# Sums of weight blocks for eight tiles of the second FFN made in HBM by accumulating transfers, and three more of its tiles by seven block products

## The chip, the cores and the metric

The kernel runs on one core of a Trainium2 chip. The metric is the device time of one execution in microseconds (us). The core's engines are named as in the profile: PE (TensorE, matrix products), PEld (its weight loads), DVE (VectorE), ACT (ScalarE), POOL (GpSimd) and SP (SyncE, which here only issues transfers). [...]

## The reference

A decoder trunk of two layers over 512 tokens of width 1024, all in float32. Layer 0 mixes tokens with a gated unit (mixer A), layer 1 with windowed attention (mixer B). Each layer then has a gated FFN with a short causal convolution, and an embedding added through a gate. What the change touches is the up projection of the FFN, `xn @ w_up`:

```python
def conv_ffn(xn, w_up, conv_w, conv_b, w_down):
    S = xn.shape[1]
    h = xn @ w_up                                   # (512, 1024) @ (1024, 5632)
    hp = jnp.pad(h, ((0, 0), (CONV_WIDTH - 1, 0), (0, 0)))
    c = conv_b + sum(hp[:, t:t + S] * conv_w[t] for t in range(CONV_WIDTH))
    g, u = jnp.split(c, 2, axis=-1)
    return (jax.nn.silu(g) * u) @ w_down
```

## The kernel before, in words

**Precision.** Every weight block is split into two float32r parts, `wh` (a cast on ACT, L203) and `wl` (the rest, a subtraction on DVE, L204), and so is every activation. A product is three matmuls: high by high, high by low, low by high (`mm3`, L224).

**Weights on their way.** All weight loads are a list of *pieces* in order of use, up to 1 MB each, and each piece is cut into *units* of up to 1024 columns (`plan` and its kin, L73 to L117). `load` (L168) issues a piece's transfer from SP into one of three staging buffers r0 to r2 of 8 KB per partition, taken in turn (`staged`, L149). `pump` (L179) splits units into four rotating pairs `wh`, `wl`, so splits run four units ahead of PE. A load therefore waits until the buffer three places back has been split. SP works in order: whatever waits on SP holds the loads behind it.

**FFN tiles.** The up projection of each layer runs in 22 tiles, numbered from 0 (`up`, L736): tile j yields 128 gate and 128 line features for 512 tokens. A plain tile has eight blocks of inputs by two outputs, 48 matmuls of 512 columns, and two units. A *woven* tile (`woven_up`, L786) pairs input blocks, cuts the tokens in halves, and forms the 2 x 2 block product with seven products instead of eight (Winograd's form of Strassen's scheme): 84 matmuls of 256 columns. For that it needs four blocks of the weights (0 to 3) and four sums of them. `weave` (L155) makes the sums on DVE into a second staging buffer (L163 to L165): s3 = w1 + w3, s0 = w1 + w0, s2 = s3 + w0, s1 = s2 + w2. A woven tile has three full units and a half one: (w0, w2), (s2, s3), (s0, s1), (w3). The products collect in two PSUM tiles `ux` and `uy`; ACT copies parts of them out (`head`, `side`, `tail`), DVE combines these (L811, L812), and `gated` (L753) applies convolution, silu and the product of gate and line. The copy `side` (L804) must be done before the last product into `uy` may begin, as that writes over it.

`UPS` lists the woven tiles, the same for both layers; `ASIDE` gives some of them another place in SBUF for `head` and `tail`.

**Order in an FFN.** `PARTS` cuts the tiles in (0, 8), (8, 16), (16, 22). Of the first two parts the down projection is woven too (`woven_add`, L593): it takes the part's activations and adds its results onto rows `saved` in HBM by accumulating transfers from POOL (L600). The first tile of the next part is computed ahead of it. So the order is: tiles 0 to 8, down projection, tiles 9 to 16, down projection, tiles 17 to 21, down projection.

**Before the FFN of layer 0**: mixer A's gate in four chunks (`u`, L1026 to L1047), its output projection (`woven_add` onto h), the embedding's projection (`ple_in`).

**Order on a queue.** Instructions are put in each engine's order by the framework; `behind(a, b)` (L143) adds that a comes after b in the order, without a wait.

Of the kernel before, what the change touches and what calls it, by code (L numbers as in the profile page):

```python
# [8 lines left out]
F32 = mybir.dt.float32  # L9
F32R = mybir.dt.float32r  # L10
AF = mybir.ActivationFunctionType
ALU = mybir.AluOpType

P = 128
D = 1024
S = 512
KD = D // P
# [2 lines left out]
NJ = FF // P  # L20
PARTS = [(0, 8), (8, 16), (16, 22)]
WOVEN = 2
UPS = (7, 8, 9, 10, 12, 14, 16, 17, 18, 20, 21)
ASIDE = {7: 12, 9: 7, 17: 7, 20: 6}
PAIRS = 4
SLOTS = 9
N = S // 2
# [25 lines left out]
def tile_yoco(ctx: ExitStack, tc: tile.TileContext, t, out: bass.AP, out_b: bass.AP):  # L53
    nc = tc.nc
# [9 lines left out]
    dram = ctx.enter_context(tc.tile_pool(name="dram", bufs=1, space=bass.MemoryType.DRAM))  # L64
# [3 lines left out]
        return mmp.tile([P, S], F32, tag="mm", name=name)  # L68


    pieces, paired, woven, beside = [], set(), set(), set()

    def plan(ap_, n, cols, own=None):  # L73
# [23 lines left out]
    def plan_woven(w, n_chunks, k0, k1):  # L97

        for c in range(n_chunks):
            n = (k1 - k0) * P  # L100
            woven.add(len(pieces))
            pieces.append((w[c, :, k0 * 256 : k1 * 256], 2 * n, [(0, n)] * 3 + [(0, n // 2)], None))

    def plan_ups(l, j0, j1):
        for j in range(j0, j1):
            (plan_woven if j in UPS else plan_cols)(t["w_up"][l, j : j + 1], 1, *((0, KD) if j in UPS else (KD,)))

    def plan_ffn(l):
        plan(t["pT"][l], 2 * S, S, own=[(mp, "m4", "m5")])
# [30 lines left out]
    raws, ready, splits, sums = {}, {}, {}, {}  # L140
    state = {"raw": 0, "unit": 0, "next": 0, "tags": [0, 1, 2], "turn": 2, "pt": 0, "sent": {}}

    def behind(ins, front):  # L143

        tc.add_manual_dep(ins.ins, front.ins.name,
                          mybir.DependencyInfo(mybir.DependencyClass.NoSync, mybir.DependencyReason.DATA),
                          reason="order")

    def staged(name):  # L149
        tags = state["tags"]  # L150
        r = wp.tile([P, 2 * UNIT], F32, tag=f"r{tags[state['turn'] % len(tags)]}", bufs=1, name=name)
        state["turn"] += 1
        return r

    def weave(i, q):  # L155


        n = pieces[i][1] // 4
        g = raws[i][:, : 4 * n].rearrange("p (k b m) -> p b k m", b=4, m=P)
        if q == 0:  # L160
            s = sums[i] = staged(f"wsum{i}")[:, : 4 * n].rearrange("p (b k m) -> p b k m", b=4, m=P)
            k = n // P
            nc.vector.tensor_add(s[:, 0::3], g[:, 1:2].to_broadcast([P, 2, k, P]), g[:, 0::3])  # L163
            nc.vector.tensor_add(s[:, 2], s[:, 3], g[:, 0])
            nc.vector.tensor_add(s[:, 1], s[:, 2], g[:, 2])  # L165
        return (g[:, 0:3:2], sums[i][:, 2:4], sums[i][:, 0:2], g[:, 3:4])[q]

    def load(upto, queue=nc.sync):  # L168
        while state["raw"] < min(upto, len(pieces)):
            j = state["raw"]  # L170
            a, m = pieces[j][:2]
            r = raws[j - 1][:, UNIT:] if j in beside else staged(f"wraw{j}")
            ins = queue.dma_start(r[:, :m].rearrange("p (c m) -> p c m", c=2) if j in paired else r[:, :m], a)
            for front in state["sent"].pop(j, []):
                behind(ins, front)
            raws[j] = r
            state["raw"] += 1
# [107 lines left out]
    minus_half = const.tile([P, S // 64], F32, name="minus_half")  # L285
# [37 lines left out]
    class Norm:  # L323
# [121 lines left out]
        def rstd(self):  # L445

            r = tp.tile([P, S], F32, tag="rstd", name=f"{self.name}rstd")
            if self.line is not None:
                nc.gpsimd.dma_start(r, self.line.partition_broadcast(P))
            else:  # L450
                nc.scalar.copy(r, self.spread(0, S // 64))
            return r

    def inv_root(ms, name, scale=1.0, n=None):
        if n is None:
            n = ms.shape[1]
            ms = [(slice(None), ms)]
        m = const.tile([P, n], F32, tag=f"ms{n}", bufs=2, name=f"{name}m")
        for some, x in ms:
            box["m"] = nc.vector.tensor_scalar(m[some, :], x, scale, EPS, op0=ALU.mult, op1=ALU.add)  # L460
        r = const.tile([P, n], F32, tag=f"rt{n}", bufs=2, name=f"{name}rt")
        nc.gpsimd.tensor_tensor(r, m, minus_half[:, :n], op=ALU.pow)
        return r

    box = {}
# [263 lines left out]
    def ffn(l, norm, nxt):  # L729
# [4 lines left out]
            behind(nc.sync.dma_start(saved[k], h[k]), box["squared", k])  # L734

        def up(j, later=False):  # L736
            if j in UPS:
                return woven_up(j, later)
            parts = chunk(256, KD)
            pss = [psum(f"up{j}_{s}") for s in range(2)]  # L740
            if j:
                for s in range(2):
                    mm3(pss[s], parts, xs, s * P)
            else:
                for k, ((wh, wl, off), (xh, xl)) in enumerate(zip(parts, xs)):
# [40 lines left out]
        def woven_up(j, later):  # L786

            product = products(ins)
            n = PAIRS * P
            chain, other = psum(f"ux{j}")[:, first], psum(f"uy{j}")  # L790
            if j in ASIDE:
                head, tail = couple(ASIDE[j], f"out{j}", F32)
            else:
                head, tail = (tp.tile([P, S], F32, tag="hs", name=f"{x}{j}") for x in ("gate", "line"))
            side = tp.tile([P, N], F32, tag="sq", name=f"side{j}")
            w = unit()
            product(1, chain, w, 0)
            behind(box["silu"], nc.scalar.copy(head[:, first], chain))
            product(2, other[:, first], w, n)
            w = unit()  # L800
            product(6, chain, w, 0, first=False)
            nc.scalar.copy(head[:, second], chain)
            product(5, other[:, second], w, n)
            nc.scalar.copy(side, other[:, second])  # L804
            w = unit()
            product(7, chain, w, 0, first=False)
            minus(tail[:, second], chain)
            product(3, other[:, second], w, n, first=False)
            product(4, chain, unit(), 0, first=False)
            minus(tail[:, first], chain)  # L810
            nc.vector.tensor_sub(tail[:, second], tail[:, second], side)  # L811
            nc.vector.tensor_add(head, head, other)  # L812
            return (head, tail) if later else gated(j, (head, tail))
# [7 lines left out]
        ins = inputs()  # L821
# [202 lines left out]
    edge = at.tile([P, PAIRS, 2, N], F32R, tag="vtl", name="edge")  # L1024
    us = [Pair(c, edge, f"us{c}", range(3 * PAIRS)) for c in range(PAIRS)]
    for c in range(4):  # L1026
        parts = chunk(256, KD)
        ups = [psum(f"u{c}_{j}") for j in range(2)]
        for j in range(2):
            mm3(ups[j], parts, xs, j * P)  # L1030
        for j in range(2):
            m = 2 * c + j
            ps = ups[j]
            z = tp.tile([P, S], F32, tag="hs", name=f"uz{m}")
            nc.vector.tensor_mul(z, ps, rstd)
            u = tp.tile([P, S], F32, tag="sg", name=f"u{m}")
            nc.scalar.activation(u, z, AF.Gelu_apprx_tanh)
            sp = psum(f"s{m}")
            for b in range(NC):
# [596 lines left out]
```

## Time and profile before

| | us |
|---|---|
| median of 3 runs (lowest to highest) | 1100.68 (1100.63 to 1100.82) |
| the profiled execution | 1100.31 |
| its span, first to last instruction | 1098.6 |
| mean granted clock of PE | 0.998 |

Where the parts of the kernel lie in the profiled execution, by the chain of waits:

| stretch | us from the span's start |
|---|---|
| mixer A's gate, four chunks | 49.8 to 98.7 |
| first FFN, tiles 0 to 8 | 153.7 to 252 |
| first FFN, tiles 9 to 16 | 290.8 to 375 |
| second FFN, tiles 9 to 16 | 838.6 to 923 |

How to read the profile: a row of the chain of waits or of the timeline has the start, the length, engine and line, and a count of instructions merged into it. A row of a group has line, engine and operation, output and inputs with shapes, count, then busy time, mean ns of one, idle time of the engine just before and what ended it. Matmuls are pipelined: their length in a group (389 ns for 512 columns, 283 for 256) is longer than the time from one to the next, so PE's cost is read from starts in the chain. A few matmul records can be missing from a trace. In a timeline a row of SP gives the issue of transfers, not their arrival.

### The profile page before, as it was taken

Reading aid. Unit: us, or ns where it says so; the run is one execution under the profiler, and the core shown is the slowest. Engines: PE = TensorE matmul, PEld = TensorE weight load, DVE = VectorE, ACT = ScalarE, POOL = GpSimd, SP = SyncE. Lnnn points to the kernel's source line nnn. Section 1 sums busy time; section 2 is a strip of 40 time slices with the busy share of each in tenths; the row PEclk is TensorE's granted clock in tenths of the full one; section 3 lists DMA queues with packets and bytes.
Section 4 is the critical chain, followed back from the end, with each engine's and each line's share of the span. In section 5 each row is a group of like instructions: output and inputs, shape, how many; then the busy total and the mean of one; then the engine's idle time right before and its main releaser. Section 6 shows DMA issues by size and latency. Waiting matters only on the chain.

```text
span 1098.6 us, 17575 instructions
## 1 busy us (share of the span) xinstructions
PE 1089.3 (99%) x6629; PEld 975.0 (89%) x6629; DVE 943.0 (86%) x1504; ACT 674.2 (61%) x1177; POOL 155.9 (14%) x228
## 2 busy tenths in 40 slices
PE   9999999999999999999999999999999999999997
PEld 7888988899998999988888887888999989999886
DVE  5598889999799978877988997799997999798886
ACT  5744666566676656655656775565666666567544
POOL 1200300002200030021114452000022000300200
PEclk9999999999999999999999999999999999999999
DMA  8621884126833388353224216441268333974534
GB/s 291 136 89 44 200 265 150 42 77 135 193 115 116 91 185 242 121 190 112 66 88 135 78 58 226 176 153 39 77 155 172 115 116 92 204 224 145 201 94 98
DMA packets 52693, 151.33 MB, mean 138 GB/s; under 512 B 13624, under 2 KB 21568, under 8 KB 42112
## 3 DMA queue, kind: packets, MB, share of 16 engines
q1 hardware_dynamic: 40560, 128.77, 36.3%
q0 software_dynamic: 10480, 16.78, 10.1%
q10 hardware_dynamic: 1568, 4.65, 1.1%
q8 instruction: 52, 0.85, 0.3%
q14 instruction: 33, 0.27, 0.1%
HBM read 116.89 MB, written 25.18 MB: 129 GB/s over the span
## 4 chain that ended last, share of the span: by engine, by line
PE 91%; DVE 3%; SPq 2%; issue 2%; ACT 1%; DMA 1%; POOL 0%; POOLq 0%; DVEq 0%; ACTq 0%
PE up L234 20%; PE ux L234 10%; PE dx L234 10%; PE uy L234 8%; PE dy L234 8%; PE q L234 4%; PE gate L234 4%; PE u L234 4%; PE o L234 4%; PE d L234 4%; PE up L749 2%; SPq L1393 2%; PE pv L1325 1%; PE v L244 1%; PE v L246 1%
## 5 line engine op out<-in xcount | busy, mean ns | idle before, releaser
L204 DVE TENSOR_TENSOR wl<-wraw,wh 128x1024 fp32r<-128x1024 f32 (+2 forms) x198 | 217.5, 1104 | 42.3 <-ACT wh L203 40.9
L203 ACT CAST wh<-wraw 128x1024 fp32r<-128x1024 f32 (+2 forms) x197 | 182.9, 933 | 108.2 <-PE up L234 21.8
L204 DVE TENSOR_TENSOR wl<-wsum,wh 128x1024 fp32r<-128x1024 f32 x84 | 102.4, 1227 | 38.1 <-ACT wh L203 37.3
L203 ACT CAST wh<-wsum 128x1024 fp32r<-128x1024 f32 x84 | 87.9, 1051 | 42.9 <-PE uy L234 14.5
L600 POOL DMA_DIRECT2D saved<-side x16 | 14.0, 873 | 404.2 <-ACT side L556 404.2
L761 DVE SCALAR_TENSOR_TENSOR c<-up,vec,c 128x511 f32<-128x511 f32 (+1 forms) x88 | 65.1, 745 | 2.4 <-ACT c L759 2.0
L234 PE MATMUL up<-nf10h,wh 128*128 128x512 f32 x160 | 62.3, 389 | 0.0
L234 PE MATMUL up<-nf00h,wh 128*128 128x512 f32 x160 | 62.3, 389 | 0.0
L234 PE MATMUL up<-nf10l,wh 128*128 128x512 f32 x160 | 62.3, 389 | 0.0
L234 PE MATMUL up<-nf00l,wh 128*128 128x512 f32 x160 | 62.3, 389 | 0.0
L234 PE MATMUL up<-nf00h,wl 128*128 128x512 f32 x160 | 62.1, 389 | 0.0
L234 PE MATMUL up<-nf10h,wl 128*128 128x512 f32 x160 | 62.0, 389 | 0.0
L759 ACT ACTIVATE c<-up,vec 128x512 f32<-128x512 f32 x44 | 34.0, 777 | 31.7 <-PE up L234 26.5
L163 DVE TENSOR_TENSOR wsum<-wraw 128x1024 f32<-128x1024 f32 x42 | 51.3, 1221 | 0.7
L234 PE MATMUL ux<-t,wh 128*128 128x256 f32 x264 | 50.4, 283 | 0.0
L234 PEld LDWEIGHTS ux<-t,wh 128*128 128x128 f32 x264 | 41.2, 192 | 0.0
L234 PE MATMUL ux<-t,wl 128*128 128x256 f32 x132 | 37.4, 283 | 0.0
L234 PEld LDWEIGHTS up<-nf10h,wl 128*128 128x128 f32 x160 | 30.0, 188 | 6.2
L234 PEld LDWEIGHTS up<-nf00h,wl 128*128 128x128 f32 x160 | 30.0, 188 | 6.2
L234 PEld LDWEIGHTS up<-nf10l,wh 128*128 128x128 f32 x160 | 30.1, 188 | 6.2
L234 PEld LDWEIGHTS up<-nf00l,wh 128*128 128x128 f32 x160 | 30.0, 188 | 6.1
L767 ACT ACTIVATE a<-c 128x512 f32<-128x512 f32 x44 | 27.8, 632 | 12.4 <-DVE c L761 12.4
(772 smaller groups left out, 3769.2 us busy)
## 6 DMA issues: line engine op xcount, KB each, us to landing
wraw<-in_w_up SPq DMA_DIRECT2D x44, 1024.0 KB, 5.4
wraw<-in_w_down SPq DMA_DIRECT2D x16, 1024.0 KB, 4.9
wraw<-in_w_gate SPq DMA_DIRECT2D x8, 1024.0 KB, 5.4
wraw<-in_w_down SPq DMA_DIRECT2D x8, 768.0 KB, 4.4
wraw<-in_w_u SPq DMA_DIRECT2D x4, 1024.0 KB, 9.4
wraw<-in_w_out SPq DMA_DIRECT2D x4, 1024.0 KB, 5.1
saved<-head POOLq DMA_DIRECT2D x16, 256.0 KB, 4.6
saved<-rest POOLq DMA_DIRECT2D x16, 256.0 KB, 6.9
```

What stands on the lines that cost most here:

```text
L163: nc.vector.tensor_add(s[:, 0::3], g[:, 1:2].to_broadcast([P, 2, k, P]), g[:, 0::3])
L203: cast = nc.scalar.copy(hi, src)
L204: state["split"] = splits[u] = cast, nc.vector.tensor_sub(low, src, hi.bitcast(F32))
L234: return [nc.tensor.matmul(ps, w, x, start=first and j == 0, stop=last and j == len(todo) - 1, skip_group_check=onto) for j, (w, x) in enu ...
L244: nc.tensor.matmul(ps, xh[:, s], wh[:, a:b], start=st, stop=False)
L246: nc.tensor.matmul(ps, xh[:, s], wl[:, a:b], start=False, stop=en)
L600: box["onto"] = nc.gpsimd.dma_start(x, y, accum_op=ALU.add)
L749: nc.tensor.matmul(ps, w[:, off + s * P : off + (s + 1) * P], x, start=k == 0 and x is xh and w is wh, stop=k == KD - 1 and x is xl)
L759: nc.scalar.activation(c, ps, AF.Identity, bias=v("conv_b", l * 2 * NJ + col), scale=cw[2])
L761: ins = nc.vector.scalar_tensor_tensor(c[:, tap:], ps[:, : S - tap], cw[2 - tap], c[:, tap:], op0=ALU.mult, op1=ALU.add)
L767: box["silu"] = nc.scalar.activation(a, cs[0], AF.Silu)
L1393: nc.sync.dma_start(y[SQ * b : SQ * (b + 1), :, a, :], x[SQ * a : SQ * (a + 1), b::NQ].rearrange("p b m d -> p b (m d)"))
```

## The change

It concerns tiles 9 to 16 of layer 1, "the second FFN".

1. Tiles 11, 13 and 15 of layer 1 become woven: `UPS` and `ASIDE` now have an entry per layer. All of tiles 9 to 16 are woven then. `head` and `tail` of 11, 13 and 15 get places 7, 12 and 12.
2. The sums of the weights of tiles 9 to 16 of layer 1 are not made on DVE any more. They are made in HBM, ahead of time, in three batches (tiles 9 and 10; 11 to 13; 14 to 16). For each batch there are six steps: two copies (w1 into s3 and s0) from SP; two accumulates (w3 and w0) from POOL; a copy s3 to s2; an accumulate w0; a copy s2 to s1; an accumulate w2. Each transfer covers all rows of a batch: 256 or 384 rows of 2 KB, read from the weights in runs of 512 bytes. Copies are put behind the last weight load in SP's order, accumulates behind POOL's last root or row transfer.
3. The steps are issued where a key comes up: `("u", c)` before chunk c of mixer A's gate, `("up", 0, j)` before tile j of the first FFN. Batch 1 lies at u 1, u 2, u 3 (two steps) and tile 2 (two); batch 2 at tiles 2, 3, 4 (two), 6 (two); batch 3 at tiles 10, 11, 12 (two), 14 (two).
4. The load of such a tile takes two staging buffers and four transfers instead of one: blocks 0 and 2 of the weights (512 KB in runs of 512 bytes), s2 and s3 (512 KB), s0 and s1 (512 KB), block 3 (256 KB in runs of 512 bytes). `weave` then only hands out views.

```diff
-UPS = (7, 8, 9, 10, 12, 14, 16, 17, 18, 20, 21)
-ASIDE = {7: 12, 9: 7, 17: 7, 20: 6}
+UPS = [(7, 8, 9, 10, 12, 14, 16, 17, 18, 20, 21), (7, 8, 9, 10, 11, 12, 13, 14, 15, 16, 17, 18, 20, 21)]
+ASIDE = [{7: 12, 9: 7, 17: 7, 20: 6}, {7: 12, 9: 7, 11: 7, 13: 12, 15: 12, 17: 7, 20: 6}]
+BATCHES = [
+    (1, 9, 11, [("u", 1), ("u", 2), ("u", 3), ("u", 3), ("up", 0, 2), ("up", 0, 2)]),
+    (1, 11, 14, [("up", 0, 2), ("up", 0, 3), ("up", 0, 4), ("up", 0, 4), ("up", 0, 6), ("up", 0, 6)]),
+    (1, 14, 17, [("up", 0, 10), ("up", 0, 11), ("up", 0, 12), ("up", 0, 12), ("up", 0, 14), ("up", 0, 14)]),
+]
...
+    def sums_ahead(l, j0, j1, keys):
+        n = KD // 2 * P
+        whole = dram.tile([(j1 - j0) * P, 4 * n], F32, name=f"sums{l}_{j0}")
+        w = t["w_up"][l, j0:j1].rearrange("j p (k b m) -> (j p) k b m", b=4, m=P)
+        s = {x: whole[:, i * n : (i + 1) * n].rearrange("r (k m) -> r k m", m=P) for i, x in enumerate((2, 3, 0, 1))}
+        for j in range(j0, j1):
+            far_sums[l, j] = whole[(j - j0) * P : (j - j0 + 1) * P]
+
+        def copy(x, y):
+            behind(nc.sync.dma_start(x, y), state["loaded"])
+
+        def onto(x, y):
+            behind(nc.gpsimd.dma_start(x, y, accum_op=ALU.add), box["onto"])
+
+        steps = [lambda: [copy(s[x], w[:, :, 1]) for x in (3, 0)],
+                 lambda: [onto(s[x], w[:, :, x]) for x in (3, 0)],
+                 lambda: copy(s[2], s[3]), lambda: onto(s[2], w[:, :, 0]),
+                 lambda: copy(s[1], s[2]), lambda: onto(s[1], w[:, :, 2])]
+        for key, step in zip(keys, steps):
+            to_come.setdefault(key, []).append(step)
+
+    def come(*key):
+        for step in to_come.pop(key, []):
+            step()
...
         n = pieces[i][1] // 4
+        if i in summed:
+            a, c = raws[i]
+            return (a[:, : 2 * n].rearrange("p (k b m) -> p b k m", b=2, m=P),
+                    a[:, 2 * n :].rearrange("p (b k m) -> p b k m", b=2, m=P),
+                    c[:, : 2 * n].rearrange("p (b k m) -> p b k m", b=2, m=P),
+                    c[:, 2 * n : 3 * n].rearrange("p (b k m) -> p b k m", b=1, m=P))[q]
...
+            if j in summed:
+                n = m // 4
+                x, y = raws[j] = staged(f"wraw{j}"), staged(f"wsum{j}")
+                for there, here in ((x[:, : 2 * n].rearrange("p (k m) -> p k m", m=P),
+                                     a.rearrange("p (k m) -> p k m", m=P)[:, 0::2]),
+                                    (x[:, 2 * n :], summed[j][:, : 2 * n]),
+                                    (y[:, : 2 * n], summed[j][:, 2 * n :]),
+                                    (y[:, 2 * n : 3 * n].rearrange("p (k m) -> p k m", m=P),
+                                     a.rearrange("p (k m) -> p k m", m=P)[:, 3::4])):
+                    state["loaded"] = queue.dma_start(there, here)
+                state["raw"] += 1
+                continue
...
         def up(j, later=False):
-            if j in UPS:
+            come("up", l, j)
+            if j in UPS[l]:
                 return woven_up(j, later)
```

More of the change, by code (lines that the diff above doesn't have):

```diff
@@ L68, in psum, with behind @@
         return mmp.tile([P, S], F32, tag="mm", name=name)
+    def behind(ins, front):
+        tc.add_manual_dep(ins.ins, front.ins.name,
+                          mybir.DependencyInfo(mybir.DependencyClass.NoSync, mybir.DependencyReason.DATA),
+                          reason="order")
     pieces, paired, woven, beside = [], set(), set(), set()
@@ L102, in plan_woven @@
             pieces.append((w[c, :, k0 * 256 : k1 * 256], 2 * n, [(0, n)] * 3 + [(0, n // 2)], None))
+    summed, far_sums, to_come = {}, {}, {}
+    def sums_ahead(l, j0, j1, keys):
[18 more added lines that the diff above has]
+            step()
+    for batch in BATCHES:
+        sums_ahead(*batch)
     def plan_ups(l, j0, j1):
         for j in range(j0, j1):
-            (plan_woven if j in UPS else plan_cols)(t["w_up"][l, j : j + 1], 1, *((0, KD) if j in UPS else (KD,)))
+            if (l, j) in far_sums:
+                summed[len(pieces)] = far_sums[l, j]
+            (plan_woven if j in UPS[l] else plan_cols)(t["w_up"][l, j : j + 1], 1,
+                                                       *((0, KD) if j in UPS[l] else (KD,)))
     def plan_ffn(l):
@@ L141, in tile_yoco @@
     state = {"raw": 0, "unit": 0, "next": 0, "tags": [0, 1, 2], "turn": 2, "pt": 0, "sent": {}}
[L143 to L147, printed above, removed]
     def staged(name):
@@ L171, in load @@
             a, m = pieces[j][:2]
+            if j in summed:
[10 more added lines that the diff above has]
+                continue
             r = raws[j - 1][:, UNIT:] if j in beside else staged(f"wraw{j}")
             ins = queue.dma_start(r[:, :m].rearrange("p (c m) -> p c m", c=2) if j in paired else r[:, :m], a)
+            state["loaded"] = ins
             for front in state["sent"].pop(j, []):
@@ L448, in rstd @@
             if self.line is not None:
-                nc.gpsimd.dma_start(r, self.line.partition_broadcast(P))
+                box["onto"] = nc.gpsimd.dma_start(r, self.line.partition_broadcast(P))
             else:
@@ L461, in inv_root @@
         r = const.tile([P, n], F32, tag=f"rt{n}", bufs=2, name=f"{name}rt")
-        nc.gpsimd.tensor_tensor(r, m, minus_half[:, :n], op=ALU.pow)
+        box["onto"] = nc.gpsimd.tensor_tensor(r, m, minus_half[:, :n], op=ALU.pow)
         return r
@@ L790, in woven_up @@
             chain, other = psum(f"ux{j}")[:, first], psum(f"uy{j}")
-            if j in ASIDE:
-                head, tail = couple(ASIDE[j], f"out{j}", F32)
+            if j in ASIDE[l]:
+                head, tail = couple(ASIDE[l][j], f"out{j}", F32)
             else:
@@ L1026, in tile_yoco @@
     for c in range(4):
+        come("u", c)
         parts = chunk(256, KD)
```

## The prediction

> **What bounds the kernel now.** I read the page's busy times first, then the chain of waits, then the stretch in which the second FFN computes its tiles 9 to 16, then what feeds that stretch. A reading aid for all of it: tile numbers count from 0, as in the code.
>
> ```profile
> span 1098.6 us, 17575 instructions
> PE 1089.3 (99%) x6629; PEld 975.0 (89%) x6629; DVE 943.0 (86%) x1504; ACT 674.2 (61%) x1177; POOL 155.9 (14%) x228
> 838.00:922.00 84.00, 84.00 (x570) 77.57 (x569) 80.70 (x117) 55.71 (x91) 1.76 (x2) 1.00 0.36 110
> ```
>
> The third line is the stretch of tiles 9 to 16, in the order length, PE, weight load, DVE, ACT, POOL, clock, DMA share, GB/s. PE never pauses for long there; DVE is at 80.70 of 84.00 (96%), ACT at 66%, DMA at a third. So the stretch ends when PE has issued its matmuls, and DVE has 3.3 us to spare in all of it. The chain of waits gives the price of each tile (start, length, matmuls):
>
> ```profile
> 838.60 1.44 PE ux L234 x12
> ...
> 845.78 1.59 PE uy L234 x12
> 847.38 2.87 PE ux L234 x24
> ...
> 855.99 0.47 PE up L234 x2
> 856.46 1.59 PE uy L234 x12
> ...
> 859.48 10.46 PE up L234 x46
> 869.94 1.43 PE ux L234 x12
> ...
> 879.99 10.91 PE up L234 x48
> 890.91 1.43 PE ux L234 x12
> ...
> 898.09 0.47 PE up L234 x2
> ...
> 901.59 10.46 PE up L234 x46
> 912.05 1.43 PE ux L234 x12
> ...
> 919.23 0.24 PE dx L234 x2
> 919.47 0.23 PE dy L234 x2
> ...
> 922.72 1.18 PE dx L234 x10
> ```
>
> A seven-product tile is ux and uy (84 matmuls of 256 columns), an eight-product one is up (48 of 512 columns). Tiles 11, 13, 15 are up: 0.47 + 10.46, 10.92 (879.99 to 890.91), 0.47 + 10.46, together 32.78. The others lie between: the stretch from 838.60 to 922.72, less the 0.47 of dx and dy issued early, is 83.65, so tiles 9, 10, 12, 14, 16 took 50.87, a mean of **10.17** (12 took 10.05, the others 10.2). Twelve matmuls cost 1.44, so 84 would cost 10.06; the rest is the step to uy that takes 1.59.
>
> **The change part by part.**
>
> Matmuls: three tiles go from 10.93 to 10.17. Eight tiles of 10.17 are 81.39, against 83.65: **-2.26 us**. At tile 12's 10.05 it would be -3.25; at 10.28 (the uy step late by twice as much in every tile) -1.4.
>
> DVE and ACT in the same stretch, one row a kind:
>
> ```profile
> L163 DVE TENSOR_TENSOR wsum<-wraw 128x1024 f32<-128x1024 f32 x5 | 6.1, 1219 | 0.0
> L164 DVE TENSOR_TENSOR wsum<-wsum,wraw 128x512 f32<-128x512 f32 x5 | 3.4, 683 | 0.0
> L204 DVE TENSOR_TENSOR wl<-wsum,wh 128x1024 fp32r<-128x1024 f32 x10 | 12.2, 1221 | 2.6 <-ACT wh L203 2.6
> L204 DVE TENSOR_TENSOR wl<-wraw,wh 128x512 fp32r<-128x512 f32 x5 | 3.4, 689 | 1.1 <-ACT wh L203 1.1
> L812 DVE TENSOR_TENSOR gate<-gate,uy 128x512 f32<-128x512 f32 x3 | 2.0, 680 | 0.0
> L811 DVE TENSOR_TENSOR line<-line,side 128x256 f32<-128x256 f32 x3 | 1.3, 419 | 0.0
> L203 ACT CAST wh<-wsum 128x1024 fp32r<-128x1024 f32 x10 | 10.5, 1052 | 8.0 <-DVE wsum L164 3.4 <-PE uy L234 3.0 <-PE up L234 1.5
> L804 ACT COPY side<-uy 128x256 f32<-128x256 f32 x5 | 1.8, 365 | 0.0
> ```
>
> DVE loses the sums of five tiles: 5 x (1.22 + 0.68 + 0.68) = 12.9 (L165 adds the same shape as L164). Each of tiles 11, 13, 15 brings one more full split (1.22), a half one (0.69) and the two combining operations (0.68 + 0.42): 3.0, three times 9.0. DVE: 80.7 - 12.9 + 9.0 = 76.8 in 81.7, 94%. That is worth nothing by itself, since DVE lay under PE; with the sums kept it would be 80.7 + 9.0 + 3 x 2.6 = 97, beyond PE. ACT gets per tile one cast of 1.05, a half one (I take 0.6, its length in elements being half), and five evacuations of 256 columns at 0.37: 3.5, three times 10.5, so 66 of 81.7, 81%. ACT stays under PE as a total; where it can be late is the first rival.
>
> Loads of tiles 9 to 16: four transfers instead of one, 1.75 MB instead of 1.0, two staging buffers instead of one plus sums (for the odd tiles instead of one). SP has the time for three more issues. Do the bytes arrive in 10.17?
>
> ```profile
> q1 hardware_dynamic: 40560, 128.77, 36.3%
> q0 software_dynamic: 10480, 16.78, 10.1%
> wraw<-in_w_up SPq DMA_DIRECT2D x44, 1024.0 KB, 5.4
> 975.26 2.12 SPq L847 DMA_DIRECT2D back<-kept  x4
> back<-kept SPq DMA_DIRECT2D x8, 512.0 KB, 6.6
> saved<-head POOLq DMA_DIRECT2D x16, 256.0 KB, 4.6
> ```
>
> The plain queue moves 128.77 MB in 36.3% of the span: 0.323 MB/us when all engines work on it, so 1.75 MB take 5.7. The rows of back<-kept are the nearest thing to the new pattern: four transfers of 512 KB issued within 2.1 us, landing 6.6 after issue, 2 MB in about 8.7, so 1.75 MB in 7.6. The 0.75 MB in runs of 512 B may go at half the rate: 3.3 + 4.9 = 8.2. All below 10.17: hidden by PE's work on the tile before. I take 8.
>
> [...]
>
> The sums ahead: three batches, each of four plain copies from SP and four accumulating transfers from POOL, of 512 KB (first batch) or 768 KB. What hides them is POOL's idle time and SP's lead over the splits:
>
> ```profile
> 106.25 0.96 POOL L600 DMA_DIRECT2D h<-side  x1 [51.23 <-ACT side L556]
> 255.46 0.92 POOL L600 DMA_DIRECT2D saved<-side  x1 [106.33 <-ACT side L556]
> 379.40 0.86 POOL L600 DMA_DIRECT2D saved<-side  x1 [86.03 <-ACT side L556]
> L600 POOL DMA_DIRECT2D saved<-side x16 | 14.0, 873 | 404.2 <-ACT side L556 404.2
> L600 POOL DMA_DIRECT2D saved<-head x16 | 13.9, 867 | 19.3 <-ACT head L703 19.3
> 281.46 10.48 SPq L173 DMA_DIRECT2D wraw<-in_w_up  x2
> 323.61 7.78 SPq L173 DMA_DIRECT2D wraw<-in_w_up  x2
> 353.75 10.46 PE up L234 x46
> ```
>
> POOL is free for 51, 106 and 86 us just where the batches lie, so nothing of POOL's own is queued behind a waiting accumulate, unless a batch runs into 106, 255 or 379. On SP a copy that waits for an accumulate holds every weight load behind it. The tightest is batch 3: its first copies follow tile 10's load (281.46), its last copy follows tile 14's (323.61) and stands before tile 15's (about 331). Its price: an accumulate of 768 KB is 0.87 of POOL, 0.786 / 0.151 = 5.2 of transfer by q0's rate and some 2 of latency (4.6 landing for 256 KB less 0.87 and 1.7): 8. Copies: 1.57 MB in 4.9 + 2, later 0.786 in 2.4 + 2. Chain to the last copy: 7 + 8 + 4.4 + 8 = 27, ready at 309, before SP comes there. From the other side: POOL's 0.87 in proportion to the number of runs (1536 against 128, 10.4), and both rates halved: 12 + 23 + 7 + 23 = 65, ready at 347. Tile 15 starts on PE at 353.3 and its first split (1.05 + 1.22) and landing (5.4) must come before, so its load may be issued up to 345.5: at worst 2 us late. POOL's time doesn't grow with the bytes (side is 128 KB, head 256 KB, both 0.87), but both have 128 runs, so of runs the rows say nothing; with POOL's 10.4 and the rates of the rows the chain is 46, ready at 328. I take between 27 and 46, and no hold either way. Batch 2 lies where all tiles have eight products, in 106 us of idle POOL, batch 1 has transfers a third smaller; all three cost nothing.
>
> [...]
>
> **Sum.** The profiled execution took 1100.31 (span 1098.6 and 1.7 around it): 1100.31 - 2.26 = 1098.05. The median of the runs is 0.37 higher, so **1098.4**. What comes after the stretch hangs on PE and shifts with it. A change under 0.2% (2.2 us) is what a measurement of this kernel can't tell from none; the forecast stands at that bound.
>
> **Rivals.**
>
> *ACT takes the place of PE's matmuls, in small pieces.* In a seven-product tile the uy step waits for the copy of side, and this stands on ACT behind a cast of 1.05 (the 1.59 for 1.44 is that wait). With ACT at 81% instead of 66% a split of an activation may stand before it too. At 0.2 more a tile, 8 x 0.2 = 1.6, 1100.0: within 0.2%. For: the 1.59 in four of five tiles now. Against: ACT's total leaves 15 us.
>
> *The feed becomes the bound: slower.* Place: the loads of tiles 9 to 16, two short-run transfers in each. If a tile's 1.75 MB take longer than 10.17 (under 172 GB/s), PE waits in each. Were all bytes at half the rate (0.162 MB/us), 10.8 a tile: 8 x 0.63 - 2.26 = +2.8, 1103.5. It decides from 10.45 a tile on. For: the accumulates into saved still run while tiles 9 and 10 are fetched. Against: 0.36 DMA share now, and the lead of a tile and a half that three staging buffers give. [...]
>
> *SP is held by a copy that waits for an accumulate: slower.* From a chain of 66 us on it costs more than is won. With accumulates at a quarter of q0's rate (20.8 and 10.4 and 2, 33 each): 12 + 33 + 7 + 33 = 85, tile 15's load at 367 instead of 345.5 at latest: +21.5 - 2.26, 1119.9. Against: it needs four times the cost of the trace's nearest rows.
>
> *The work isn't what bounds:* that DVE's relief itself frees PE can't be, since PE has no wait there but the uy steps; at most those vanish, 1097.4, the far end of the forecast.
>
> **How the numbers follow.** Forecast 0.75 (1097.4 to 1099.3: -3.25 to -1.4 from the median), ACT 0.09, feed 0.09, held SP 0.07. Of the forecast 0.6 lies beyond 0.2%: faster 0.45; same 0.30 + 0.08 = 0.38; slower 0.17. The range takes in the forecast, the ACT case, the 2 us of a late tile 15 and the beginning of the feed case: 1097.2 to 1101.5.
>
> **What would show it.** Right: tiles 11, 13, 15 as ux and uy with about 10.2 each, the stretch from tile 9 to 16 81.4 long, DVE 77 and ACT 66 in it, no PE wait on a load; POOL done with its accumulates before 106, 255 and 379; SP's loads of tiles 6 to 16 of the first FFN where they are now. Wrong: PE or ACT idle until wraw or the second half of a staged pair lands (feed), a PE gap in the first FFN behind tiles 13 to 16 (held SP), or uy steps above 1.7 (ACT).

## The result, and the profile after

The changed kernel takes 1109.24 us (median of 6 runs, 1107.79 to 1111.97) against 1100.66 for the kernel before on the same chip: a ratio of 1.0078, 95% interval 1.0068 to 1.0088. It is slower by 8.6 us, where 1098.4 was forecast and 1101.5 was the upper end.

The profiled execution was the longest of the six, 1111.97 with a span of 1110.3. The page of the changed kernel, its span, the engines' busy time and the accumulating queue:

```profile
span 1110.3 us, 17897 instructions
PE 1092.4 (98%) x6737; PEld 982.9 (89%) x6737; DVE 939.4 (85%) x1501; ACT 681.3 (61%) x1198; POOL 178.3 (16%) x240
q0 software_dynamic: 27056, 25.17, 16.1%
```

No engine has become a bound over the whole; that queue moves 8.4 MB more and DVE is a little less busy. The loss sits in two places, and neither is where the forecast looked for one.

**First loss: tiles 7 and 8 of the first FFN, which the change does not touch.** Two views by tile, first and last start of PE's rows: the first matmul of tile 7 (`ux`), and the first `dx` of the down projection behind tile 8, of before and then of the changed kernel.

```profile
L234 PE MATMUL ux<-nf00h,wh x8: 278/283/283, 229.7 to 240.9; 128*128 128x256 f32 x8
L234 PE MATMUL dx<-edge,wh x16: 278/280/284, 247.0 to 260.1; 128*128 128x256 f32 x16
```

```profile
L293 PE MATMUL ux<-nf00h,wh x8: 278/283/415, 229.4 to 245.3; 128*128 128x256 f32 x8
L293 PE MATMUL dx<-edge,wh x8: 278/280/284, 251.4 to 255.9; 128*128 128x256 f32 x8
```

17.3 us have become 22.0. SP's issues ahead of it (start, time from the first issue of the row to the end of its last), before:

```profile
155.95 54.82 SPq L173 DMA_DIRECT2D wraw<-in_w_up  x6
```

and in the changed kernel, where L128 are the copies of the sums and L231 the weight loads:

```profile
156.12 9.44 SPq L231 DMA_DIRECT2D wraw<-in_w_up  x2
180.24 0.50 SPq L128 DMA_DIRECT2D sums<-sums  x1
180.84 1.81 SPq L231 DMA_DIRECT2D wraw<-in_w_up  x2
198.20 0.50 SPq L128 DMA_DIRECT2D sums<-sums  x1
198.81 18.10 SPq L231 DMA_DIRECT2D wraw<-in_w_up  x2
```

Two copies of batch 2 (s2 from s3, s1 from s2) stand on SP until an accumulate has landed. The waits of SP from 140 to 250 (total, times, longest):

```profile
SPq L128 <- DMA sums<-in_w_up: 30.1, 2, 15.5
```

So the load of tile 7 went out at 198.81; before it was the fifth of its row, at 188.49. It took 8.8 to land, where the loads of that row took 4.9 to 5.9 before: the batch keeps the DMA engines busy too (a share of 0.83 from 188 to 199, 0.28 before), but the 10.3 of waiting on SP are the larger part. DVE's rows of the first sum of that tile and of a later split, before:

```profile
201.46 1.21 DVE L163 TENSOR_TENSOR wsum<-wraw 128x1024 f32<-128x1024 f32 x1
228.03 1.23 DVE L204 TENSOR_TENSOR wl<-wsum,wh 128x1024 fp32r<-128x1024 f32 x1 [0.51 <-ACT wh L203]
```

and in the changed kernel:

```profile
207.73 1.22 DVE L209 TENSOR_TENSOR wsum<-wraw 128x1024 f32<-128x1024 f32 x1 [6.45 <-DMA wraw<-in_w_up]
232.59 1.21 DVE L263 TENSOR_TENSOR wl<-wsum,wh 128x1024 fp32r<-128x1024 f32 x1
```

DVE stands 6.45 us for the load and is 6.3 late at the sum; 25 us on it is still 4.6 late. The stretches around tile 7 in the changed kernel (length, PE, weight load, DVE, ACT, POOL, clock, DMA share, GB/s):

```profile
229.40:240.00 10.60, 7.84 (x63) 7.41 (x62) 10.60 (x17) 7.56 (x14) 0.00 (x0) 1.00 0.30 100
240.00:246.00 6.00, 6.00 (x39) 6.00 (x39) 5.33 (x8) 3.58 (x7) 0.00 (x0) 0.72 0.20 44
```

and before:

```profile
229.40:240.00 10.60, 10.60 (x89) 10.47 (x88) 9.36 (x14) 7.20 (x12) 0.00 (x0) 1.00 0.28 100
```

DVE is busy in all of the 10.60 us and PE works in 7.84 of them. So a load held at 188 to 199 is paid 30 us later, by PE, as soon as the woven tiles need all of DVE. Behind the pauses the granted clock falls to 0.72.

**Second loss: tile 9 of the second FFN.** The chain of waits of the changed kernel there, and at the end of tile 16:

```profile
836.12 12.29 DMA wsum<-in_w_up
...
850.00 2.93 PE ux L293 x12
852.93 2.56 PE uy L293 x12
855.49 1.57 PE ux L293 x12
...
932.85 1.18 PE dx L293 x10
```

Tile 9 began at 842.5, 4.1 later than before (838.4), which is the first loss. The `dx` behind tile 16 starts at 932.85 against 922.72, 10.13 later. So the stretch has lost another 6.0 instead of winning 2.26. The rows of ACT and the wait of PE name the cause:

```profile
844.85 1.05 ACT L262 CAST wh<-wsum 128x1024 fp32r<-128x1024 f32 x1 [4.57 <-DMA wsum<-sums]
848.79 0.62 ACT L262 CAST wh<-wsum 128x512 fp32r<-128x512 f32 x1 [2.41 <-DMA wsum<-in_w_up]
```

```profile
PE ux L293 <- ACT out9h L858: 4.4, 1, 4.4
```

ACT's casts of the second staged half of tile 9 wait 4.57 and 2.41 us for transfers, and behind them on ACT stands, at 849.59, the copy `out9h`, which empties the PSUM tile that PE wants next. PE waits 4.4 us, and then has the clock against it. The stretch of the gap and the two behind it, in the columns above:

```profile
845.30:850.00 4.70, 0.27 (x3) 0.06 (x1) 1.79 (x2) 2.29 (x6) 0.88 (x2) 0.88 1.03 260
850.00:855.00 5.00, 5.00 (x23) 5.00 (x24) 2.71 (x5) 2.09 (x4) 0.84 (x1) 0.50 0.90 181
855.00:860.00 5.00, 5.00 (x41) 5.00 (x40) 2.70 (x4) 3.24 (x5) 0.00 (x0) 0.93 0.52 178
```

Steps of twelve matmuls that take 1.44 took 2.93, 2.56 and 1.57: 2.7 us more. 4.4 + 2.7 = 7.1, of which tiles 10 to 16 win 1.1 back. Why its second half landed late stands in SP's issues:

```profile
833.39 0.58 SPq L227 DMA_DIRECT2D wraw<-in_w_up  x1
834.02 1.56 SPq L227 DMA_DIRECT2D wraw<-sums  x1
835.68 0.38 SPq L227 DMA_DIRECT2D wsum<-sums  x1
836.12 0.55 SPq L227 DMA_DIRECT2D wsum<-in_w_up  x1
```

The first two are tile 10's first half, 1 MB, issued ahead of tile 9's second half (the last two), beside accumulates onto `saved`. In the code tile 9's four transfers stand ahead of tile 10's; the order on SP is the framework's.

The profiled execution is 11.7 longer than before. Of the 1.6 us that remain, 1.2 are lost in the last gate, where weight loads land some 0.5 to 0.8 later (below).

### The profile page after: what moved, and what is told of

It reads as the page before. It is cut to its first block, busy times and chain, and to the rows that moved or that the text cites. A ratio compares the mean times of both kernels' runs of the same rounds, so it can differ in the third digit from the quotient of the medians.

```text
span 1110.3 us, 17897 instructions
## 1 busy us (share of the span) xinstructions
PE 1092.4 (98%) x6737; PEld 982.9 (89%) x6737; DVE 939.4 (85%) x1501; ACT 681.3 (61%) x1198; POOL 178.3 (16%) x240
## 4 chain that ended last, share of the span: by engine, by line
PE 70%; DVE 3%; DMA 3%; ACT 1%; issue 1%; SPq 0%; POOLq 0%; POOL 0%; ACTq 0%; DVEq 0%
PE ux L293 12%; PE up L293 11%; PE uy L293 9%; PE dx L293 8%; PE dy L293 6%; PE q L293 4%; PE gate L293 4%; PE o L293 4%; PE d L293 4%; DMA wraw<-in_w_gate 2%; PE pv L1386 1%; DMA wsum<-in_w_up 1%; PE up L809 1%; PE k L293 1%; DVE wl L263 1%
## 5 line engine op out<-in xcount | busy, mean ns | idle before, releaser
L293 PE MATMUL ux<-t,wh 128*128 128x256 f32 x300 | 59.0, 289 | 5.2 <-ACT out9h L858 4.4
L821 DVE SCALAR_TENSOR_TENSOR c<-up,vec,c 128x511 f32<-128x511 f32 (+1 forms) x76 | 56.1, 744 | 2.1 <-ACT c L819 1.6
L293 PEld LDWEIGHTS ux<-t,wh 128*128 128x128 f32 x300 | 47.8, 196 | 6.2 <-ACT out9h L858 4.6
L209 DVE TENSOR_TENSOR wsum<-wraw 128x1024 f32<-128x1024 f32 x37 | 45.1, 1220 | 7.3 <-DMA wraw<-in_w_up 6.7
L293 PE MATMUL up<-nf10h,wh 128*128 128x512 f32 x112 | 43.6, 389 | 0.0
L293 PE MATMUL up<-nf10l,wh 128*128 128x512 f32 x112 | 43.6, 389 | 0.0
L293 PE MATMUL up<-nf10h,wl 128*128 128x512 f32 x112 | 43.3, 389 | 0.0
L293 PE MATMUL ux<-t,wl 128*128 128x256 f32 x150 | 43.0, 286 | 0.0
L131 POOL DMA_DIRECT2D sums<-in_w_up x12 | 23.7, 2091 | 90.8 <-DMA sums<-sums 83.2
L293 PEld LDWEIGHTS up<-nf00h,wh 128*128 128x128 f32 x160 | 30.0, 188 | 6.0
## 6 DMA issues: line engine op xcount, KB each, us to landing
sums<-in_w_up POOLq DMA_DIRECT2D x8, 768.0 KB, 10.8
```

The lines of the kernel that those rows point to most:

```text
L131: behind(nc.gpsimd.dma_start(x, y, accum_op=ALU.add), box["onto"])
L293: return [nc.tensor.matmul(ps, w, x, start=first and j == 0, stop=last and j == len(todo) - 1, skip_group_check=onto) for j, (w, x) in enu ...
L821: ins = nc.vector.scalar_tensor_tensor(c[:, tap:], ps[:, : S - tap], cw[2 - tap], c[:, tap:], op0=ALU.mult, op1=ALU.add)
```

## The experiments

**Each loss alone.** First the sums made but read by nobody (`a_prep_only`):

```diff
-UPS = [..., (7, 8, 9, 10, 11, 12, 13, 14, 15, 16, 17, 18, 20, 21)]
+UPS = [..., (7, 8, 9, 10, 12, 14, 16, 17, 18, 20, 21)]
...
-                summed[len(pieces)] = far_sums[l, j]
+                pass
```

> The sums are made in HBM as in the changed kernel, but nobody reads them: tiles 9 to 16 of the second FFN load and multiply as before the change. Theory (two separate losses: about 4.3 us in tiles 7 and 8 of the first FFN, because SP stands at copies that wait for accumulates while weight loads wait behind them; about 6 us at tile 9 of the second FFN, because its second staged half arrives late): only the first loss is left, about 1100.7 + 4.3 = 1105, the woven tiles 7 and 8 at about 22.0 instead of 17.3, the stretch of tiles 9 to 16 of the second FFN at 84.0 as before. Rival 1 (the accumulates cost the second FFN something by themselves, say by what they leave in HBM or in the queues): more than 1106 and a longer stretch in the second FFN. Rival 2 (the loss in the first FFN comes from elsewhere, say from a shift of the schedule): about 1100.7.

Measured: 1105.26 (ratio 1.004, 1.0026 to 1.0055). The `dx` behind tile 8 follows tile 7's start by 21.3 (229.6 to 250.9), and the second FFN is as before. Only the first loss is there.

Then the loads of the change without copies or accumulates (`b_feed_only`):

```diff
-            far_sums[l, j] = whole[(j - j0) * P : (j - j0 + 1) * P]
+            far_sums[l, j] = t["w_up"][l, j]
...
-        for key, step in zip(keys, steps):
-            to_come.setdefault(key, []).append(step)
```

> No copies and no accumulates: tiles 9 to 16 of the second FFN load pieces of the weights themselves, of the same shapes and runs, where the sums would be (so seven products are made of wrong sums; the sums are left out). Theory: the loss in the first FFN is gone (tiles 7 and 8 at 17.3), the loss at tile 9 of the second FFN stays, since it comes from where its second half is staged and in what order the loads go: about 1100.7 + 6 = 1106 to 1107, tile 9 about 17 instead of 10.2. Rival (the sums were not ready, or the bytes in HBM that accumulates left behind are slower to read): tile 9 near 10.3 and about 1098.5 to 1100.

Measured: 1105.64 (1.0045, 1.003 to 1.006). Tiles 7 and 8 are at 17.4 again and tile 9 stalls as in the changed kernel (PE waits 3.7 for `out9h`), with nothing but plain reads in its loads. The chain of this kernel:

```profile
831.02 12.31 DMA wsum<-in_w_up
...
844.64 2.36 PE ux L289 x12
847.00 2.28 PE uy L289 x12
```

The two kernels lie 4.5 and 4.8 over before, 9.3 together, for the 8.6 lost (each ratio is sure to some 1.6 us): the two losses are independent, and the sums' being ready, or their place in HBM, plays no part in the second.

**The first loss: SP or the DMA engines?** The dependent copies issued by POOL (`c_copies_pool`):

```diff
+        def later(x, y):
+            behind(nc.gpsimd.dma_start(x, y), box["onto"])
...
-                 lambda: copy(s[2], s[3]), lambda: onto(s[2], w[:, :, 0]),
-                 lambda: copy(s[1], s[2]), lambda: onto(s[1], w[:, :, 2])]
+                 lambda: later(s[2], s[3]), lambda: onto(s[2], w[:, :, 0]),
+                 lambda: later(s[1], s[2]), lambda: onto(s[1], w[:, :, 2])]
```

> The two copies of each batch that wait for an accumulate are issued by POOL, behind that accumulate, instead of by SP; bytes and transfers are the same. Theory (SP stands at them): SP no longer waits, tiles 7 and 8 of the first FFN at 17.3 to 18, first loss gone, second stays: 1109.2 - 4.3 = about 1105. Rival (contention: the DMA engines are full of accumulates with short runs, so that weight loads land late whatever queue issues them): tiles 7 and 8 stay at about 22, 1109.

Measured: 1104.92 (1.0041, 1.0027 to 1.0055). SP issues its six loads from 156.09 on in one row of 54.21, as before, and PE has no pause in tile 7:

```profile
229.40:240.00 10.60, 10.60 (x90) 10.55 (x90) 9.84 (x14) 7.47 (x13) 0.00 (x0) 1.00 0.30 100
```

The same bytes cost nothing there, though single loads of that row now took up to 16.7 to land: they went out early enough, and DVE waits for none of them between 140 and 300. It was SP's place in line that made the loss.

**Which batch?** Batch 1 dropped (`d_no_batch1`), and batch 1 dropped with batch 2 in its place (`e_early`):

```diff
-    (1, 9, 11, [("u", 1), ("u", 2), ("u", 3), ("u", 3), ("up", 0, 2), ("up", 0, 2)]),
```

```diff
-    (1, 9, 11, [("u", 1), ("u", 2), ("u", 3), ("u", 3), ("up", 0, 2), ("up", 0, 2)]),
-    (1, 11, 14, [("up", 0, 2), ("up", 0, 3), ("up", 0, 4), ("up", 0, 4), ("up", 0, 6), ("up", 0, 6)]),
+    (1, 11, 14, [("u", 1), ("u", 2), ("u", 3), ("u", 3), ("up", 0, 2), ("up", 0, 2)]),
```

> The first batch (tiles 9 and 10) is dropped: these two tiles load plain and DVE makes their sums as before; tiles 11 to 16 as in the changed kernel. Theory: the loss at tile 9 is gone, as tile 9 needs one buffer that is free early and DVE's sums are done ahead; the stall may come back smaller at tile 11, the first with two buffers, but a tile and a half of lead is then there. The loss in tiles 7 and 8 of the first FFN is smaller or the same, since the second batch's first copies come there too: if batch 1 causes all of it, 1100.7 - 2 = 1098.7; if batch 2 causes all of it, about 1103. Rival (the second loss is a matter of feed in every summed tile, and stands at the first of them whichever it is): a gap of 4 to 5 us at tile 11, about 1104 to 1109.

> As without the first batch, but the second batch (tiles 11 to 13, 768 KB a transfer) takes the first one's place: in the second, third and fourth pass over u and behind tile 1 of the first FFN. Theory (it is the place: the copies that wait stand on SP between the loads of tiles 4 to 7 of the first FFN, where DVE has no slack): the loss in tiles 7 and 8 of the first FFN comes back, and with half as many runs again in each accumulate it is as large or larger, 4 to 7 us: about 1100.7 + 4 to 7 = 1104.5 to 1107.5. Rival (it is the sum of two batches close together; one alone in that place does nothing): tiles 7 and 8 at 17.3, about 1100.5.

Measured: 1100.65 and 1100.64 (both 1.0001, 0.9992 to 1.001). Neither place does harm with one batch in it; the expectation for `e_early` missed by 4 us, and its rival held. In `d_no_batch1` there is no stall at tile 9, which loads plainly, nor at tile 11, now the first with two staged halves; but the 2 us that its expectation added as a gain are not there either. In `d_no_batch1` SP still stands at batch 2's copies, but sooner and for less:

```profile
170.04 0.52 SPq L127 DMA_DIRECT2D sums<-sums  x1
...
190.21 0.50 SPq L127 DMA_DIRECT2D sums<-sums  x1
190.81 19.90 SPq L230 DMA_DIRECT2D wraw<-in_w_up  x2
```

Its longest hold there is 10.7 and tile 7's load goes out at 190.81; with both batches these were 15.5 and 198.81. With batch 1's last copy (148.02) and accumulate ahead of it, batch 2's first accumulate starts at 166.00 on POOL instead of 159.72, and its chain ends 8 us later. Spacing the batches (`k_apart`, made with the transfers in order, next paragraph) tests that:

```diff
-    (1, 11, 14, [("up", 0, 2), ("up", 0, 3), ("up", 0, 4), ("up", 0, 4), ("up", 0, 6), ("up", 0, 6)]),
+    (1, 11, 14, [("up", 0, 4), ("up", 0, 5), ("up", 0, 6), ("up", 0, 6), ("up", 0, 8), ("up", 0, 8)]),
```

> All three batches and the four transfers of a tile in order, copies on SP; the second batch is moved two tiles later (behind tiles 4 to 8 of the first FFN, instead of 2 to 6), so that its first copies and accumulates come when the first batch is done. Theory as the runs have left it (two batches close together: they share the DMA engines, so each accumulate takes longer, and SP stands longer at the copy behind it than DVE's lead over PE lasts): the longest hold of SP falls from 15.5 to under 8, tiles 7 and 8 of the first FFN go back from 19.7 to 17.3, 1102.85 - 2.35 = 1100.5. Rival (the second batch is then too near to the third, which begins behind tile 10): the gap moves to tiles 10 to 14, 1103 to 1110.

Measured: 1100.88 (1.0001, 0.9991 to 1.001). All three batches are there, tiles 7 and 8 are at 17.3, and tile 7's load goes out at 188.78. The one hold between 140 and 250 is 8.2, a shade over what was expected, and it ends just when the load behind it could go anyway (188.49 before). The load took 9.8 to land, which is 198.6 and still ahead of DVE's sum at 201.5.

**The second loss: order or contention?** The four transfers of a tile put in order, tile 9's second half ahead of tile 10's first (`f_in_order`):

```diff
-                    state["loaded"] = queue.dma_start(there, here)
+                    ins = queue.dma_start(there, here)
+                    behind(ins, state["loaded"])
+                    state["loaded"] = ins
```

> All three batches as in the changed kernel, but each of a tile's four transfers is put behind the load before it in SP's order, so that the second half of tile 9 goes ahead of tile 10's first half. Theory in its first form (tile 9's second half lands late because 1 MB of tile 10 is issued ahead of it): it lands some 3 to 4 us earlier, the gap at tile 9 shrinks from 4.7 to under 1.5, and the clock does not fall behind it: 1109.2 - 4 to 6 = 1103 to 1105, with the loss in tiles 7 and 8 of the first FFN left as it was. Second form (it lands late because its buffer comes free late, and because accumulates onto saved fill the DMA engines then): the gap stays at 3 to 5, 1107 to 1109.

Measured: 1102.85 (1.0027, 1.0016 to 1.0038); only the first loss remains, here 2.3 of the median. In the profile SP's longest hold is 15.3, much as in the changed kernel, but PE's waits come to 2.1 instead of 2.7 and the clock stays at 1.00 behind them: tile 7's start to the first `dx` is 19.7 instead of 22.0. SP now issues tile 9's second half first:

```profile
833.67 0.33 SPq L227 DMA_DIRECT2D wsum<-sums  x1
834.04 0.58 SPq L227 DMA_DIRECT2D wsum<-in_w_up  x1
834.68 0.74 SPq L227 DMA_DIRECT2D wraw<-in_w_up  x1
```

and ACT waits for no transfer between 832 and 862. The first form of the theory holds. The two transfers go out only 0.5 sooner ahead of tile 9's start (7.3 for 6.8), but land after 5.6 and 6.6 instead of 9.1 and 12.3, with nothing but the order changed. That tile 10's 1 MB, now behind them, is what had slowed them is the author's reading. The stretch of eight seven-product tiles can now be read without a stall. From this kernel's chain:

```profile
841.12 1.44 PE ux L295 x12
...
870.48 2.87 PE ux L295 x24
...
879.57 1.58 PE uy L295 x12
...
891.04 2.87 PE ux L295 x24
...
924.27 1.18 PE dx L295 x10
```

870.48 to 891.04 are two tiles: 10.28 each. The stretch is 924.27 - 841.12 - 0.47 = 82.68, against 83.65 before: 0.97 won, not 2.26.

**Both remedies together.** Copies on POOL and transfers in order (`g_pool_and_order`, the two edits above), and the batches later with transfers in order (`i_later_order`):

```diff
-    (1, 9, 11, [("u", 1), ("u", 2), ("u", 3), ("u", 3), ("up", 0, 2), ("up", 0, 2)]),
-    (1, 11, 14, [("up", 0, 2), ("up", 0, 3), ("up", 0, 4), ("up", 0, 4), ("up", 0, 6), ("up", 0, 6)]),
+    (1, 9, 12, [("up", 0, 2), ("up", 0, 3), ("up", 0, 4), ("up", 0, 4), ("up", 0, 6), ("up", 0, 6)]),
+    (1, 12, 14, [("up", 0, 7), ("up", 0, 8), ("up", 0, 9), ("up", 0, 9), ("up", 0, 10), ("up", 0, 10)]),
```

> Both remedies at once: the dependent copies issued by POOL and the four transfers of a tile in order. If the two losses are independent and both remedies hold: 1104.9 - 4 to 6 = 1099 to 1101, tiles 7 and 8 of the first FFN at 17.3, the stretch of tiles 9 to 16 of the second FFN at about 82.3 to 83 (three tiles at 10.27 for 10.92). If the order is no remedy: about 1104 to 1105.

> The sums of all eight tiles as in the changed kernel, but with the batches later: tiles 9 to 11 behind tiles 2 to 6 of the first FFN, 12 and 13 behind its tiles 7 to 10, 14 to 16 where they were; and the four transfers of a tile in order. Theory: as with no first batch the place behind tiles 2 to 6 costs nothing, so the first loss is gone with the copies still on SP; if the order is a remedy 1099 to 1101, if not about 1104 to 1105. Rival (more than two batches in tiles 2 to 14 leave SP held somewhere else): a gap in tiles 9 to 16 of the first FFN.

`g_pool_and_order`: 1101.08 (1.0008, 0.9999 to 1.0017), both losses gone but for 1.0 us of PE at tile 9: there a load of tile 10 took 11.41 to land (issued 831.65), and ACT's cast of it stood before `out9h`. Here the loads fit beside the accumulates onto `saved` with little to spare.

`i_later_order`: 1111.1 (1.0093, 1.0079 to 1.0108), a miss by 10 us and the rival's case; the profiled execution, 1107.67, was the shortest of its five. Batches 2 and 3 are now too near each other, SP's longest hold is 13.7, and the first FFN's tile 12 pays. The issue of its load, its DVE row, its wait of PE and its stretch:

```profile
305.76 1.02 SPq L233 DMA_DIRECT2D wraw<-in_w_up  x1
```

```profile
318.65 1.23 DVE L209 TENSOR_TENSOR wsum<-wraw 128x1024 f32<-128x1024 f32 x1 [8.11 <-DMA wraw<-in_w_up]
```

```profile
PE ux L295 <- ACT gate L860: 5.7, 1, 5.7
```

```profile
330.00:335.60 5.60, 5.44 (x25) 5.44 (x26) 5.43 (x10) 3.31 (x7) 0.00 (x0) 0.50 0.84 219
```

DVE is late at its sums and PE waits 5.7, as in the first loss, and then has half the clock (0.50; there it was 0.72). But the hold is the smaller part here. The load went out at 305.76, against 303.09 before, and then took 12.9 to land instead of 4.9. Between 300 and 312 the DMA share was 1.34 at 178 GB/s, before it was 0.33 at 98. So the batches near each other also slowed the weight load beside them, and whether copies on POOL would have helped in this place was not tried.

**What is left of the gain.** `before_again` is the kernel before, profiled once more:

> The kernel before, once more, for the spread of one place: every changed kernel has the first 36 matmuls of the last gate in 8.4 to 9.3 instead of 8.18. If that is the chip's spread, this profile shows 8.4 or more too; if it belongs to the change, 8.2.

The first 36 matmuls of the last gate took 8.16 (8.18 in the first profile), 1100.32 in all. So it isn't the chip's spread: in the kernels with any part of the change they took 8.4 to 9.3. The gate's loads from 1018 on land later in them; the landing times (least, median, most) of `d_no_batch1` and of `before_again`:

```profile
DMA to landing us min/median/max: 5.7/6.0/6.2
```

```profile
DMA to landing us min/median/max: 5.2/5.3/5.5
```

No run isolates why: `b_feed_only` without accumulates (8.72) and `a_prep_only` without the new loads (8.48) both have it. It takes back 0.2 to 0.7 of the 0.97, and the rest is inside the intervals of 1.0001.

The uy step is late in each seven-product tile, for the copy `side` stands on ACT behind a cast. `l_side_first` is `e_early` with that copy first, in every woven tile of both layers; `m_before_side_first` is the same edit on the kernel before:

```diff
             w = unit()
+            if state["next"] + 2 in splits:
+                behind(splits[state["next"] + 2][0], aside)
             product(7, chain, w, 0, first=False)
```

> The kernel with the first batch dropped and the second in its place, and in every woven tile of both layers ACT copies side ahead of the cast that has stood before it. Theory (the seven-product tiles take 10.27 and not 10.05 because the uy step waits for that copy): uy steps of 1.59 go to 1.44, a pair of tiles from 20.55 to 20.2 or less, some 0.1 to 0.2 in each of 25 woven tiles: 1100.6 - 2.5 to 5 = 1095.5 to 1098. Rival (the cast that now comes later delays DVE and with it PE by as much): 1100 to 1102.

> The kernel before, with ACT's copy of side put ahead of the cast in every woven tile, and nothing else. If what the last run won (1 us) is that order alone, this one wins as much or more: 1099 to 1099.8. If the order pays only together with tiles 11, 13 and 15 at seven products (there the uy step is late in every tile), it is within 0.4 of before: 1100.3 to 1101. If it delays DVE, which is at 96% in tiles 9 to 16 of this kernel, it is slower: 1101 to 1103.

Measured: 1099.75 (0.9989, 0.998 to 0.9998) and 1099.56 (0.9992, 0.9983 to 1.0001). The uy steps are at 1.44, as expected, but in `l_side_first` PE then waits elsewhere (steps of 24 matmuls at 3.01 and 3.04 where 2.87 is the price), so 1 us came instead of 2.5 to 5. The kernel before with the edit alone does as well. The two can't be told apart, so nothing measurable of that 1 us is due to the three tiles.

## Why the prediction was wrong

**The matmuls (-2.26): right in kind, mis-sized.** Tiles 11, 13 and 15 are ux and uy, at 10.28 and not 10.17. The text had 10.28 as its other end, -1.4, for a uy step late by twice as much; that is what steps like the 1.58 above show. At tile 16 a further wait of 0.5 for `side` leaves -0.97 over the stretch. So the first rival, ACT in small pieces, was there along with the forecast, at about 1.3 where its price was 1.6.

**DVE and ACT totals: right.** 76.8 and 66 were forecast for 81.7 us. In `f_in_order`, 81.7 us of the stretch have:

```profile
840.50:922.20 81.70, 81.25 (x667) 80.01 (x665) 77.17 (x115) 63.31 (x111) 1.76 (x2) 1.00 0.64 195
```

**"Hidden by PE's work on the tile before": the step that failed second, worth +7 at one tile.** The rate was judged, and the rate was sufficient: in `f_in_order` tiles run at 10.28 with 1.75 MB each. Nor did runs of 512 bytes show the half rate allowed for them: in the changed kernel 512 KB in such runs landed 4.6 after issue in the median, 512 KB of sums 5.7 (s2, s3) and 4.3 (s0, s1). What was not asked is which transfer comes first on SP, and when the buffer of tile 9's second half comes free. Tile 9 has the down projection before it, so its second buffer is late, and 1 MB of the next tile was let past. The "lead of a tile and a half" does not exist at the first tile of a part. The second rival named the accumulates onto `saved` beside tiles 9 and 10, but as a wait in every tile at 0.63. That rival's sum was also too small by the text's own figures: twice 5.7 is 11.4 a tile and not 10.8, so 8 x 1.23 - 2.26 = +7.6 and not +2.8.

**"Batch 2 lies where all tiles have eight products ... all three cost nothing": the step that failed first, worth +4.3.** The held SP was a rival, with the right mechanism and the wrong place. Only batch 3 was worked out. Its chain was forecast at 27 to 46, the last copy at 328 by POOL's rows; it was issued at 330.16, ahead of tile 15's load at 335.56, and cost nothing, as said. Batch 2 was dismissed in a clause, though it runs against tile 7, which is woven and has sums on DVE, and though batch 1 ends where batch 2 begins. Its 768 KB accumulates hold SP for up to 15.5. The 8 of the text was too little: they landed 10.8 after their issue in the median, and 14.2 and 14.5 where batch 2 meets batch 1. So was the 7 for a batch's first copies: those of batch 2 took 17.1 and 19.8. The upper case of 33 for an accumulate (quarter rate) wasn't needed. The deadline was wrong too: PE's start of a tile less one split. DVE makes a woven tile's sums long before PE gets there (201.5 for tile 7, which PE starts at 229.7), and what it lost there was not made up in time: of 6.3 us 4.6 were still missing 25 us later, with DVE busy in 24.63 of the 24.90 from 207.7 to 232.6.

**The clock: not in the text at all.** A pause of PE was priced at its own length. At tile 9 4.4 us of waiting brought 2.7 of half clock, in `i_later_order` 5.7 brought 2.8 (2.93, 2.56 and 1.65 for steps of 1.44).

**The lists of what would show it** did their work: SP's loads of tiles 6 to 16 were to stay where they were, and did not; PE or ACT idle until the second half of a staged pair lands was a sign of a wrong forecast, and appeared. The third, a PE gap behind tiles 13 to 16 of the first FFN, didn't appear: the held SP struck elsewhere.

## What to carry to other kernels

A transfer that waits, put on a queue that also feeds the tightest engine, is priced by the next load behind it and by the first engine that consumes that load, not by the engine that sets the end: here SP's hold of 15.5 became 6.45 of waiting on DVE and 4.7 more in PE's tiles 7 and 8. Add what such transfers cost the loads beside them (in `i_later_order` one took 12.9 to land instead of 4.9). Batches placed one behind the other are to be timed as one chain. With a new stream of loads, look at the first tile after another kind of work: which buffer is free when, and which transfer goes first. Where PE will have a pause, ask for the clock behind it too: here it cost 2.7 more behind a wait of 4.4 and 2.8 behind one of 5.7. Behind waits of 2.7 (changed kernel) and 2.1 (`a_prep_only`) in tile 7 the clock fell as well, behind 2.1 in `f_in_order` it did not.

## What the runs showed of the hardware

The accumulating transfers landed later than weight loads (10.8 in the median for 768 KB, loads of 1024 KB 5.9; the first plain copies of a batch, 768 KB too, took 15.6), and were dearer to issue than those onto `saved`. The issues of 768 KB with their median time to landing, and POOL's group of all twelve (busy, mean ns, idle before):

```profile
sums<-in_w_up POOLq DMA_DIRECT2D x8, 768.0 KB, 10.8
L131 POOL DMA_DIRECT2D sums<-in_w_up x12 | 23.7, 2091 | 90.8 <-DMA sums<-sums 83.2
```

An accumulate of 256 KB with 128 runs cost POOL 0.87 before, these with 1024 or 1536 runs some 2: more, but far from in proportion.

The granted clock was 0.50 in the 5 us behind a pause of 4.7 (tile 9) and in the 5.6 behind a wait of 5.7 (`i_later_order`), and back at 0.93 in the next 5. Matmuls were 0.12 apart again 5.7 (tile 9) and 5.9 us (`i_later_order`) after PE had resumed. And the clock was also at 0.72 in tile 7, behind two waits of PE of 1.9 and 0.8, and at 0.74 in the same 6 us of `a_prep_only`, behind 1.9 and 0.2, but at 1.00 in `f_in_order`, behind 2.1. So behind waits that add up to 2.7 and to 2.1 the clock fell, and behind others of 2.1 it did not; what decides it these runs don't show.
